# The delta rule's last group with its two pairs of heads interleaved, modulation sums moved out of the output projection's last quarter, and the feed-forward input scaled in another place

## The chip, the cores and the metric

The kernel runs on one core of a Trainium2 chip. The metric is device microseconds of one execution; lower is better. TensorE (PE) does the matmuls; its weight loads are listed apart as PEld. VectorE (DVE), ScalarE (ACT) and GpSimd (POOL) do the elementwise work. SyncE (SP), ACT and POOL issue DMA transfers, each in its own order. Every engine works through its instructions in a fixed order, and waits at an instruction until the semaphores it names have been reached.

## The reference, cut to what matters

One layer of a hybrid encoder block for one sequence of 256 tokens and a model width of 2048, all in fp32:

```python
mod = c_act @ ada_w + ada_b
shift_m, scale_m, gate_m, shift_f, scale_f, gate_f = split(mod, 6)
h = rms_norm(x, norm_mix_w) * (1 + scale_m) + shift_m
proj = h @ w_in                                  # all branch inputs and the merge gates
y_a = (sigmoid(a_o) * norm(bidirectional(mlstm, ...))) @ w_branch_a
y_b = (norm(bidirectional(gated_delta, ...)) * silu(b_z)) @ w_branch_b
x = x + gate_m * ((g_a * y_a + g_b * y_b) @ w_out)
hf = rms_norm(x, norm_ffn_w) * (1 + scale_f) + shift_f
gt, up = split(hf @ w_gate_up, 2)
x = x + gate_f * ((silu(gt) * up) @ w_down)
return rms_norm(x, norm_final_w)
```

The gated delta rule has 16 heads of width 128, the mLSTM 4 heads; the feed-forward is 5632 wide.

## The kernel before

**Weights.** Every projection is a job of the generator `tjob` or `fjob`. A weight tile `raw` of 1 MB is loaded by SP into one of 4 buffers, and in halves of 128x1024 it is split into a rounded part `wh` (ACT) and a remainder `wl` (DVE), with 3 buffers each. PE multiplies wh with the high and the low part of the input, and wl with the high part: 12 matmuls of 128x512 for each half. Each `next` of such a job issues one half. In names, o3_2_0 is the half from row 0 of weight tile 2 of job o3. The jobs for the merge gates are ma0 to ma3 and mb0 to mb3, those of the mLSTM branch a, v and o, those of the branch outputs ya and yb, the output projection is once more called o (o0 to o3, one for each quarter of the columns, its weights are `wo`), and the feed-forward has gt, up and d.

**The delta rule.** The 16 heads go in four groups of four, each as two pairs. `gdn_phase2(g, p)` is a generator of nine steps for one pair: p1 to p4 (small matmuls that invert blocks, each followed by DVE and ACT work), pa, pb and pc (matmuls with the triangular blocks, each followed by a scaling on ACT or a subtraction on DVE), po (12 matmuls, then a norm: squares on ACT, a root, four scalings `on` on DVE), and px (transposes, evicted by ACT as `obt` and stored to memory). Each step waits for the step ahead of it on another engine. Between steps the loop calls `stream` (the input projections of later heads, and behind them jobs from the list `fills`), so that PE has other work. The lists `after` and `last` say how many half-jobs go behind each step. For the last group, g = 3, the stream holds fills alone: the remaining a jobs and ma3.

When the last group is done its pool of buffers is closed. The next stage uses the same memory, so its first instructions wait for the last pair's stores: `obh` and `obl` (the delta rule's output o4_0 to o4_3, read back from memory and split by ACT and DVE), the branch projection yb, and POOL's loads for the mLSTM (`mkq`, `vt`, `sgo`, `bc`, two heads ahead), which stand behind its load of o4_3. psc is the mLSTM's first matmul, pden and ph follow.

**Modulation sums.** `mod` is not computed on PE. For each block of 128 outputs, SP loads a 1 MB tile `ada` and one DVE instruction (line 127) multiplies it with the conditioning row and sums it up. The parts 2 to 5 of these sums are a background list: `sums(n)` issues n of them, and `pump`, called once for each weight tile of a job, issues one at every `every[0]`-th call. Part 4 (the feed-forward's scale) must be complete before `affn`, which scales the feed-forward's input. In the projection o, sums are issued behind chosen halves of each quarter.

**Into the feed-forward.** The last quarter of o finishes token block 0 first and then token block 1. For each, DVE does tm = acc_o * gm and x1 += tm (`residual`), ACT the squares, and `token_rstd` a reduce (DVE), a root (ACT) and a reciprocal (DVE). Then `normed` scales x1 into xn, a quarter of the columns at a time and two buffers in all; `moved` transposes it on PE (pxn), scales it to `hf` (DVE, or ACT for most odd blocks) and rounds it to hfh (ACT); `low` makes hfl (DVE). The first feed-forward job, gt0, is issued in between, block pair by block pair.

Tile's scheduler places the instructions of each engine by its own model of time; those wrapped in `order(...)` keep their program order among themselves.

Of the kernel before, what the change touches and what calls it, by code (L numbers as in the profile page):

```python
# [52 lines left out]
def hybrid_block(ctx: ExitStack, tc: tile.TileContext, xr, nfr, crow, pk_d, cst_d, ada2, ada4, win0, winb, wint, wba, wbb, wo, wgu, wd, out, dbg=None):  # L53
# [809 lines left out]
    after = (0, 1, 2, 1, 2, 2, 2, 2, 4, 0)  # L863
    last = (0, 1, 2, 1, 2, 2, 1, 1, 3, 0)

# [25 lines left out]
    for g in range(4):  # L891
# [9 lines left out]
        every[0] = (0, 2, 2, 2)[g]  # L901
        for p in range(2):
            pieces = stream(4 * g + 2 * p + 4)
            if g == 3:
                o4s += [o_load(i, op, 3) for i in ((0, 1), (2,))[p]]
            for n in range(1, 10):
                next(pairs[p], None)
                if p == 0:
                    next(blocks, None)
                for _ in range(after[n] if g < 3 else last[n]):  # L910
                    next(pieces)
            for _ in pairs[p]:
                pass

            if g < 3:
                while 4 * g + 2 * p + 5 not in heads:
                    next(pieces)
        if g < 3:
# [233 lines left out]
    for g in range(4):  # L1152
# [33 lines left out]
    def normed(q, t, parts, eng):  # L1186
        if q not in xns:
            xns[q] = hp.tile([P, 2, 512], F32, tag="sg", bufs=2, name=f"xn{q}")
        o, i = xns[q][:, t, parts], x1[:, t, q * 512 + parts.start : q * 512 + parts.stop]
        if eng is V:  # L1190
            order(V.tensor_scalar(o, i, rs1[:, t : t + 1], None, ALU.mult))
        else:
            order(S.activation(o, i, AF.Copy, scale=rs1[:, t : t + 1]))
# [20 lines left out]
    for t in range(2):  # L1214
        normed(0, t, slice(256, 512), S)
    moved(0)
    moved(1)
# [5 lines left out]
    for b in range(2, KB, 2):  # L1223
# [4 lines left out]
        next(gt0)  # L1228
        if b % 4 == 2 and b < 12:
            for t in range(2):  # L1230
# [163 lines left out]
```

## Time and profile before

| | |
|---|---|
| time, median of 3 runs | 1982.52 us (1982.24 to 1983.56) |
| the profiled execution's own time | 1979.27 us |
| its span | 1977.3 us |
| mean granted PE clock | 0.988 |
| PE busy | 1918.9 us (97%) |
| PEld busy | 1705.5 us (86%) |
| DVE busy | 1402.5 us (71%) |
| ACT busy | 1022.7 us (52%) |
| POOL busy | 96.9 us (5%) |
| read from memory | 469.16 MB |

All times inside the profile count from the start of its span. The last group's first step, p1, stands at 861.69; the output projection o ends at 1253.71; the feed-forward begins at 1262.28 with gt0 and ends with the span. The granted clock is the share of TensorE's full speed that it was given.

### The profile page before, as it was taken

To read this page: it belongs to the slowest core of one execution; us is meant where nothing else is said; L and a number is where in the kernel's file an instruction comes from. 1 tells how busy PE (TensorE), PEld (TensorE's weight loads), DVE (VectorE), ACT (ScalarE), POOL (GpSimd) and SP (SyncE) were. 2 spreads that over 40 slices of the span, in tenths; PEclk is the share of its full clock that TensorE was granted. 3 is DMA by queue.
4 is the path that set the end of the run, shared out by engine and by line. 5 is a ranking of instruction groups with operands and counts; after the bars stand their busy time and mean duration, and the time that the engine had idled before them with its cause. 6 is when DMAs were issued, how large, how long until landed. Compare 5 with 4: busy or idle time off the path is not lost.

```text
span 1977.3 us, 27036 instructions
## 1 busy us (share of the span) xinstructions
PE 1918.9 (97%) x10352; PEld 1705.5 (86%) x10352; DVE 1402.5 (71%) x2091; ACT 1022.7 (52%) x1568; POOL 96.9 (5%) x185
## 2 busy tenths in 40 slices
PE   8999999999999999999799999799999999999997
PEld 6887889989989998998688888688888888888886
DVE  5779887878988996965587769766666655555554
ACT  3146657855765686465454444554444444444443
POOL 0000300110100011000200000000000000000000
PEclk9999999999999999999799999899999999999999
DMA  9996665567667765885677679466766765566563
GB/s 400 420 383 194 222 223 192 167 203 283 228 199 247 281 214 191 310 303 190 234 291 266 249 288 419 182 234 235 265 244 237 262 246 193 205 240 203 202 206 114
DMA packets 78675, 487.76 MB, mean 247 GB/s; under 512 B 10265, under 2 KB 15681, under 8 KB 23889
## 3 DMA queue, kind: packets, MB, share of 16 engines
q1 hardware_dynamic: 63360, 450.95, 62.2%
q0 software_dynamic: 7872, 19.99, 4.4%
q10 hardware_dynamic: 7314, 15.10, 2.1%
q8 instruction: 81, 1.33, 0.3%
q14 instruction: 48, 0.39, 0.1%
HBM read 469.16 MB, written 16.83 MB: 246 GB/s over the span
## 4 chain that ended last, share of the span: by engine, by line
PE 73%; DVE 11%; DMA 9%; ACT 4%; issue 2%; POOL 0%; SPq 0%; ACTq 0%; DVEq 0%; POOLq 0%
DMA ra<-ada 5%; PE acc_up L215 4%; PE acc_up L218 4%; PE acc_up L216 4%; PE acc_d L216 4%; PE acc_d L215 4%; PE acc_d L218 4%; PE acc_gt L216 4%; PE acc_gt L215 4%; PE acc_gt L218 4%; PE acc_o L218 2%; PE acc_o L216 2%; PE acc_o L215 2%; PE acc_a L175 2%; PE acc_b L175 2%
## 5 line engine op out<-in xcount | busy, mean ns | idle before, releaser
L198 DVE TENSOR_TENSOR wl_d<-raw_d,wh_d 128x1024 fp32r<-128x1024 f32 x88 | 107.8, 1225 | 102.7 <-ACT wh_d L197 102.7
L127 DVE SCALAR_TENSOR_TENSOR ada<-ada,crow 128x2048 f32<-128x2048 f32 x64 | 146.5, 2289 | 43.6 <-DMA ada<-ada 43.5
L198 DVE TENSOR_TENSOR wl_up<-raw_up,wh_up 128x1024 fp32r<-128x1024 f32 x88 | 107.5, 1225 | 95.9 <-ACT wh_up L197 95.9
L197 ACT ACTIVATE wh_d<-raw_d 128x1024 fp32r<-128x1024 f32 x88 | 93.0, 1057 | 130.5 <-PE acc_d L216 125.3
L198 DVE TENSOR_TENSOR wl_gt<-raw_gt,wh_gt 128x1024 fp32r<-128x1024 f32 x88 | 107.7, 1224 | 72.4 <-ACT wh_gt L197 68.2
L197 ACT ACTIVATE wh_gt<-raw_gt 128x1024 fp32r<-128x1024 f32 x88 | 92.9, 1056 | 120.7 <-PE acc_gt L216 73.2
L197 ACT ACTIVATE wh_up<-raw_up 128x1024 fp32r<-128x1024 f32 x88 | 93.0, 1056 | 118.2 <-PE acc_up L216 71.7
L215 PE MATMUL acc_gt<-wh_gt,hfh 128*128 128x512 f32 x352 | 135.2, 384 | 0.0
L216 PE MATMUL acc_gt<-wh_gt,hfl 128*128 128x512 f32 x352 | 134.6, 382 | 0.0
L175 PE MATMUL acc_b<-hh,wh_b 128*128 128x256 f32 x576 | 134.6, 276 | 0.0
L175 PE MATMUL acc_b<-hl,wh_b 128*128 128x256 f32 x576 | 134.6, 277 | 0.0
L215 PE MATMUL acc_up<-wh_up,hfh 128*128 128x512 f32 x352 | 133.5, 379 | 0.0
L216 PE MATMUL acc_up<-wh_up,hfl 128*128 128x512 f32 x352 | 133.5, 379 | 0.0
L216 PE MATMUL acc_d<-wh_d,ffl 128*128 128x512 f32 x344 | 130.4, 379 | 0.0
L215 PE MATMUL acc_d<-wh_d,ffh 128*128 128x512 f32 x344 | 130.4, 379 | 0.0
L530 PE MATMUL first<-x,raw 128*128 128x256 f32 x512 | 114.5, 382 | 7.5 <-ACT x L523 6.8
L530 PEld LDWEIGHTS first<-x,raw 128*128 128x128 f32 x512 | 96.1, 190 | 25.9 <-ACT x L523 12.4
L175 PEld LDWEIGHTS acc_b<-hl,wh_b 128*128 128x128 f32 x576 | 110.6, 192 | 0.4
L175 PEld LDWEIGHTS acc_b<-hh,wh_b 128*128 128x128 f32 x576 | 110.5, 192 | 0.5
L197 ACT ACTIVATE wh_o<-raw_o 128x1024 fp32r<-128x1024 f32 x64 | 67.1, 1054 | 58.9 <-PE acc_o L216 35.5
L218 PE MATMUL acc_gt<-wl_gt,hfh 128*128 128x512 f32 x352 | 95.3, 385 | 0.0
L171 ACT ACTIVATE wh_b<-raw_b 128x1024 fp32r<-128x1024 f32 x72 | 76.1, 1058 | 37.1 <-PE acc_b L175 22.8
(384 smaller groups left out, 5018.4 us busy)
## 6 DMA issues: line engine op xcount, KB each, us to landing
ada<-ada SPq DMA_DIRECT2D x64, 1024.0 KB, 5.8
raw_gt<-wgu SPq DMA_DIRECT2D x44, 1024.0 KB, 5.0
raw_up<-wgu SPq DMA_DIRECT2D x44, 1024.0 KB, 4.9
raw_d<-wd SPq DMA_DIRECT2D x44, 1024.0 KB, 4.9
raw_b<-winb SPq DMA_DIRECT2D x36, 1024.0 KB, 5.0
ra<-ada SPq DMA_DIRECT2D x32, 1025.0 KB, 15.8
raw<-win SPq DMA_DIRECT2D x16, 1024.0 KB, 17.1
raw_z<-wint SPq DMA_DIRECT2D x16, 1024.0 KB, 5.2
```

The lines of the kernel that those rows point to most:

```text
L127: V.scalar_tensor_tensor(raw, raw, 1.0, row_c[:, :D], ALU.mult, ALU.mult, accum_out=mod[:, c0 + b : c0 + b + 1])
L171: S.activation(wh, raw[:, k0 : k0 + 8], AF.Copy)
L175: PE.matmul(o, wh[:, k], both(x, k0 + k).rearrange("p a b -> p b a"), start=k0 + k + i == 0, stop=False)
L197: order(S.activation(wh, raws[u][:, k0 : k0 + 2], AF.Copy), hold)
L198: order(V.tensor_tensor(wl, raws[u][:, k0 : k0 + 2], wh.bitcast(F32), ALU.subtract), hold)
L215: order(PE.matmul(ps[t], tok(xh, kk, t), turns(wh[:, k]), start=kk == 0, stop=False), early and steps > 1)
L216: PE.matmul(ps[t], tok(xl, kk, t), turns(wh[:, k]), start=False, stop=False)
L218: PE.matmul(ps[t], tok(xh, kk, t), turns(wl[:, k]), start=False, stop=kk == last)
L530: PE.matmul(first[o], raw[:, o], x[:, b], start=b == 0 and o % 2 == 0, stop=b == KB - 1 and o % 2 == 1)
```

## The change

It has four parts.

1. In the last group the two pairs are driven by one loop of 13 rounds: the first pair takes a step in rounds 1 to 9, the second in rounds 5 to 13. Two half-jobs follow each round (26 in all, as many as with the list `last`).
2. `every[0] = 0` moves from ahead of the last ya job to behind it, so that two sums are issued within the last ya jobs.
3. In o, sums stand behind halves 2, 4, 6, 7 of the first quarter, behind 1, 3, 5, 7 of the second and third, and behind none of the last, apart from the call that empties the list there.
4. In `normed`, xn1 is made by POOL instead of ACT and issued ahead of the transposes; xn2 and xn3 are issued one pass of the loop sooner.

```diff
-    last = (0, 1, 2, 1, 2, 2, 1, 1, 3, 0)
...
-        for p in range(2):
+        for p in range(2) if g < 3 else ():
             pieces = stream(4 * g + 2 * p + 4)
-            if g == 3:
-                o4s += [o_load(i, op, 3) for i in ((0, 1), (2,))[p]]
             for n in range(1, 10):
                 next(pairs[p], None)
                 if p == 0:
                     next(blocks, None)
-                for _ in range(after[n] if g < 3 else last[n]):
+                for _ in range(after[n]):
                     next(pieces)
...
+        if g == 3:
+            flow = [stream(4 * g + 4 + 2 * p) for p in range(2)]
+            for n in range(1, 14):
+                next(pairs[0], None)
+                if n > 4:
+                    next(pairs[1], None)
+                if n < 6:
+                    next(blocks, None)
+                if g == 3 and n in (1, 6):
+                    o4s += [o_load(i, op, 3) for i in ((0, 1), (2,))[n > 1]]
...
+                for _ in range(2):
+                    next(flow[n > 8])
...
         if g == 3:
-            every[0] = 0
             while len(background) > 2:
                 sums()
             row_store(2, ml, 0.5)
         run(y_a(g, mgh, mgl))
+    every[0] = 0
...
-            if i in ((4, 6, 7), (1, 2, 4, 6), (1, 2, 4, 6), (1, 2, 4))[g]:
+            if i in ((2, 4, 6, 7), (1, 3, 5, 7), (1, 3, 5, 7), ())[g]:
                 sums()
             if g == 3 and i == 4:
                 sums(P)
...
-        if eng is V:
-            order(V.tensor_scalar(o, i, rs1[:, t : t + 1], None, ALU.mult))
+        if eng is not S:
+            order(eng.tensor_scalar(o, i, rs1[:, t : t + 1], None, ALU.mult))
...
     for t in range(2):
         normed(0, t, slice(256, 512), S)
+    for t in range(2):
+        normed(1, t, slice(0, 512), G)
     moved(0)
...
-        if b % 4 == 2 and b < 12:
+        if b % 4 == 0 and b < 12:
             for t in range(2):
                 normed(b // 4 + 1, t, slice(0, 512), S)
```

What this does to the engines' orders, at three places. In the names, 3_1 is the last group's second pair, and a trailing number is a buffer's. Lines above 860 are up to 18 higher in the changed file.

PE at the end of the merge job ma3, before: the pair's last steps stand behind the job, and the branch projection yb0 behind them.

```order
L218 MATMUL acc_ma3_1_9176<-wl_ma3_3_2_9326,hh_131 128x512
L775 MATMUL pb_3_1_8773<-z3_1_8728,gg14_7349 128x128 x2
L775 MATMUL pb_3_1_8773<-z3_1_8728,gg15_7594 128x128 x2
L763 MATMUL pc_3_1_8799<-r3_1_8729,UL_1115 128x128
L764 MATMUL pc_3_1_8799<-r3_1_8729,UL_1115 128x128
L785 MATMUL po_3_1_8826<-z3_1_8728,at14_7350 128x128
```

PE at the same place, after: from the pair's last px, inside the job's last half, to the first matmul of yb0.

```order
L796 MATMUL px_3_1_8809<-cst_78,on15_8824 128x128 x2
L215 MATMUL acc_ma3_0_9175<-wh_ma3_3_2_9325,hh_131 128x512
L216 MATMUL acc_ma3_0_9175<-wh_ma3_3_2_9325,hl_132 128x512
L215 MATMUL acc_ma3_1_9176<-wh_ma3_3_2_9325,hh_131 128x512
L216 MATMUL acc_ma3_1_9176<-wh_ma3_3_2_9325,hl_132 128x512
L218 MATMUL acc_ma3_0_9175<-wl_ma3_3_2_9326,hh_131 128x512
L218 MATMUL acc_ma3_1_9176<-wl_ma3_3_2_9326,hh_131 128x512
L218 MATMUL acc_ma3_0_9175<-wl_ma3_3_2_9326,hh_131 128x512
L218 MATMUL acc_ma3_1_9176<-wl_ma3_3_2_9326,hh_131 128x512
L215 MATMUL acc_yb0_0_9366<-wh_yb0_0_0_9370,obh_8961 128x512
```

All of the pair's matmuls now stand ahead of the job's last 8; pb, pc, po and px were 24 behind it.

DVE at the same place, before: ada3_7 is a modulation sum, r, so and on belong to the pair, obl is the next stage.

```order
L127 SCALAR_TENSOR_TENSOR ada3_7_9505,mod_88<-ada3_7_9505,crow_76 128x2048
L198 TENSOR_TENSOR wl_yb0_0_2_9387<-raw_yb0_0_9368,wh_yb0_0_2_9386 128x1024
L776 TENSOR_TENSOR r3_1_8729<-vv14_7345,pb_3_1_8773 128x256
L776 TENSOR_TENSOR r3_1_8729<-vv15_7590,pb_3_1_8773 128x256
L810 SCALAR_TENSOR_TENSOR so3_1_8840<-so3_1_8840,sm14_7322 128x2
L810 SCALAR_TENSOR_TENSOR so3_1_8840<-so3_1_8840,sm15_7567 128x2
L814 RECIPROCAL so3_1_8840<-so3_1_8840 128x4
L819 SCALAR_TENSOR_TENSOR on14_8841<-po_3_1_8826,so3_1_8840,sz3_7794 128x128 x2
L819 SCALAR_TENSOR_TENSOR on15_8842<-po_3_1_8826,so3_1_8840,sz3_7794 128x128 x2
L933 TENSOR_TENSOR obl_8962<-o4_0_8217,obh_8961 128x1024
```

DVE there, after:

```order
L819 SCALAR_TENSOR_TENSOR on14_8823<-po_3_1_8808,so3_1_8822,sz3_7794 128x128 x2
L819 SCALAR_TENSOR_TENSOR on15_8824<-po_3_1_8808,so3_1_8822,sz3_7794 128x128 x2
L198 TENSOR_TENSOR wl_ma3_3_0_9310<-raw_ma3_3_9307,wh_ma3_3_0_9309 128x1024
L198 TENSOR_TENSOR wl_ma3_3_2_9326<-raw_ma3_3_9307,wh_ma3_3_2_9325 128x1024
L198 TENSOR_TENSOR wl_yb0_0_0_9371<-raw_yb0_0_9368,wh_yb0_0_0_9370 128x1024
L127 SCALAR_TENSOR_TENSOR ada3_7_9505,mod_88<-ada3_7_9505,crow_76 128x2048
L198 TENSOR_TENSOR wl_yb0_0_2_9387<-raw_yb0_0_9368,wh_yb0_0_2_9386 128x1024
L949 TENSOR_TENSOR obl_8962<-o4_0_8228,obh_8961 128x1024
```

The pair's norm now stands ahead of the merge job's last splits. The sum ada3_7 and the split behind it, for which SP's next two raw_yb loads wait, still follow the merge job's last split.

DVE at the end of o, before: tmss is the tm of `residual`, with the token block and the quarter in its name.

```order
L1113 TENSOR_TENSOR tmss1_10970_0_3_11585<-acc_o3_0_11445,gm_10968 128x512
L127 SCALAR_TENSOR_TENSOR ada4_14_11481,mod_88<-ada4_14_11481,crow_76 128x2048
L1114 TENSOR_TENSOR x1_10966<-x1_10966,tmss1_10970_0_3_11585 128x512
L1123 TENSOR_REDUCE rs1_10971<-ss1_10970 128x1
L1125 RECIPROCAL rs1_10971<-rs1_10971 128x1
L1113 TENSOR_TENSOR tmss1_10970_1_3_11604<-acc_o3_1_11446,gm_10968 128x512
L1114 TENSOR_TENSOR x1_10966<-x1_10966,tmss1_10970_1_3_11604 128x512
L127 SCALAR_TENSOR_TENSOR ada4_15_11502,mod_88<-ada4_15_11502,crow_76 128x2048
L1123 TENSOR_REDUCE rs1_10971<-ss1_10970 128x1
L129 TENSOR_TENSOR mod_88<-mod_88,pk_77 128x16
L1167 SCALAR_TENSOR_TENSOR affn_10972<-mod_88,pk_77 128x16
L1125 RECIPROCAL rs1_10971<-rs1_10971 128x1
```

DVE there, after:

```order
L127 SCALAR_TENSOR_TENSOR ada4_15_11405,mod_88<-ada4_15_11405,crow_76 128x2048
L129 TENSOR_TENSOR mod_88<-mod_88,pk_77 128x16
L1183 SCALAR_TENSOR_TENSOR affn_10978<-mod_88,pk_77 128x16
L198 TENSOR_TENSOR wl_o3_3_0_11560<-raw_o3_3_11557,wh_o3_3_0_11559 128x1024
L198 TENSOR_TENSOR wl_o3_3_2_11564<-raw_o3_3_11557,wh_o3_3_2_11563 128x1024
L198 TENSOR_TENSOR wl_gt0_0_0_11570<-raw_gt0_0_11567,wh_gt0_0_0_11569 128x1024
L1129 TENSOR_TENSOR tmss1_10976_0_3_11585<-acc_o3_0_11452,gm_10974 128x512
L1130 TENSOR_TENSOR x1_10972<-x1_10972,tmss1_10976_0_3_11585 128x512
L1139 TENSOR_REDUCE rs1_10977<-ss1_10976 128x1
L1141 RECIPROCAL rs1_10977<-rs1_10977 128x1
L1129 TENSOR_TENSOR tmss1_10976_1_3_11604<-acc_o3_1_11453,gm_10974 128x512
L1130 TENSOR_TENSOR x1_10972<-x1_10972,tmss1_10976_1_3_11604 128x512
```

The last sum and `affn` now stand ahead of o3's last weight splits, and no sum stands among the residual's instructions.

POOL from the mLSTM's last gate row to the end, after (before, the two rows of line 1207 were not there):

```order
L141 DMA row_d2_92<-rowsm2_10794 16x128
L144 DMA gm_10974<-row_d2_92 128x2048
L1207 ISA
L1207 TENSOR_SCALAR xn1_11633<-x1_10972,rs1_10977 128x512 x2
L141 DMA row_d5_93<-rowsm5_15051 16x128
L144 DMA gf_15046<-row_d5_93 128x2048
```

[...]

More of the change, by code (lines that the diff above doesn't have):

```diff
@@ L913, in hybrid_block @@
                 pass
-            if g < 3:
-                while 4 * g + 2 * p + 5 not in heads:
-                    next(pieces)
+            while 4 * g + 2 * p + 5 not in heads:
+                next(pieces)
+        if g == 3:
[8 more added lines that the diff above has]
+                    o4s += [o_load(i, op, 3) for i in ((0, 1), (2,))[n > 1]]
+                if n == 9 and g < 3:
+                    while 4 * g + 5 not in heads:
+                        next(flow[0])
+                for _ in range(2):
+                    next(flow[n > 8])
+            for pair in pairs:
+                for _ in pair:
+                    pass
+            while g < 3 and 4 * g + 7 not in heads:
+                next(flow[1])
         if g < 3:
```

## The prediction

> **What bounds the kernel now.** I read the page first (busy shares, slices of the clock), then the windows table stage by stage, then in order of time each engine around the two places where TensorE is not busy.
>
> ```profile
> PE 1918.9 (97%) x10352; PEld 1705.5 (86%) x10352; DVE 1402.5 (71%) x2091; ACT 1022.7 (52%) x1568; POOL 96.9 (5%) x185
> ...
> PEclk9999999999999999999799999899999999999999
> ```
>
> TensorE is busy for 97% of the span; its granted clock sags in only two slices. The windows table (stretch; then length, busy time and, in brackets, count of PE, PEld, DVE, ACT, POOL; last the granted clock, the DMA share, GB/s) shows what they are:
>
> ```profile
> 860.00:934.70 74.70, 74.70 (x501) 69.78 (x500) 42.21 (x48) 44.91 (x87) 0.00 (x0) 1.00 0.66 236
> 934.70:951.77 17.07, 6.66 (x46) 5.31 (x44) 4.75 (x13) 7.82 (x21) 0.39 (x1) 0.83 0.51 171
> 951.77:965.24 13.47, 9.76 (x32) 7.11 (x32) 7.67 (x10) 5.01 (x5) 7.49 (x13) 0.83 0.96 348
> 966.40:980.06 13.66, 13.17 (x44) 11.35 (x44) 7.24 (x19) 6.16 (x10) 2.10 (x4) 0.50 0.48 160
> 1253.71:1260.51 6.80, 0.01 (x2) 0.01 (x1) 5.54 (x14) 2.49 (x8) 0.00 (x0) 0.71 0.00 0
> 1260.51:1291.57 31.06, 26.21 (x117) 21.25 (x117) 20.05 (x32) 20.55 (x36) 0.00 (x0) 0.90 0.32 105
> 1291.57:1950.00 658.43, 658.43 (x3096) 577.38 (x3095) 378.73 (x349) 294.30 (x312) 1.05 (x2) 1.00 0.65 228
> ```
>
> Until 934.70 and from 1291.57 on PE never pauses, so only these gaps can be won: 934.70 to 965.24, where the second pair's last steps stand without fill work and the mLSTM's loads follow, and 1253.71 to 1291.57, from the last output projection into the feed-forward. A full-clock 128x512 matmul comes every 658.43 / 3096 = 0.213 us.
>
> **Part 1, the pairs.** PE, ACT, POOL and SP at the first gap, in order of time (start, length; in brackets the idle time before and its releaser):
>
> ```profile
> 934.70 0.61 PE L775 MATMUL pb<-z,gg 128*128 128x128 f32 x4
> 937.56 0.68 PE L775 MATMUL pb<-z,gg 128*128 128x128 f32 x4 [2.26 <-DVE r L776]
> 941.40 0.39 PE L785 MATMUL po<-z,at 128*128 128x128 f32 x2
> 942.52 0.39 PE L790 MATMUL po<-z,at 128*128 128x128 f32 x2
> 946.25 0.73 PE L796 MATMUL px<-cst,on 128*128 128x128 f32 x2 [3.34 <-DVE on L819]
> 947.54 0.69 PE L796 MATMUL px<-cst,on 128*128 128x128 f32 x2 [0.56 <-ACT obt L798]
> 951.77 1.22 PE L215 MATMUL acc_yb<-wh_yb,obh 128*128 128x512 f32 x2 [3.53 <-ACT obh L932]
> 965.24 2.62 PE L957 MATMUL psc<-mkq 128*128 128x256 f32 x8 [3.33 <-DMA mkq<-kq_d]
> ...
> 935.62 1.08 ACT L332 ACTIVATE ev_ma<-acc_ma 128x512 f32<-128x512 f32 x2
> 950.66 2.95 ACT L932 ACTIVATE obh<-o 128x1024 fp32r<-128x1024 f32 x3 [1.92 <-DMA ob_d<-obt]
> 951.38 0.80 POOL L886 DMA_DIRECT2D o<-ob_d  x1 [100.38 <-DMA ob_d<-obt]
> 935.85 1.47 SPq L193 DMA_DIRECT2D raw_yb<-wbb  x2
> ```
>
> At 934.70 the last merge job is used up; the pair's pb, pc, po and px then wait for DVE and ACT with nothing between. The quoted orders put these 24 small matmuls among the merge job. Nothing is added; PE pays for them in time, (942.52 - 941.40) / 5 = 0.224 each, 5.4 us, so the merge job ends at 940.1. The last px now stands 8 matmuls (1.7 us) ahead of that and ends at 938.4, against 947.54 + 0.69 = 948.23 before: 9.8 us sooner. Everything that waited for the pair's store moves with it: obh followed px by 2.43 us, POOL's load of the last o by 3.15 (941.6 now). On ACT the eviction ev_ma now stands between px's eviction and obh; it needs the merge job's end and 1.1 us, so obh starts at 941.2 instead of 940.8, and PE starts yb (1.11 behind obh) at 942.3. That costs nothing: PE's next wait, for mkq, ends later.
>
> That wait is where part of the gain goes. psc needs the second mkq, behind five other loads on POOL's queue, and 951.77 to 965.24 ran DMA at a share of 0.96. Until now other traffic had passed by then:
>
> ```profile
> q1 hardware_dynamic: 252, 1.93, 64.9%
> q10 hardware_dynamic: 140, 0.52, 14.2%
> ...
> gtb<-mb_d SPq DMA_DIRECT2D x2, 512.0 KB, 4.3
> o<-ob_d POOLq DMA_DIRECT2D x1, 512.0 KB, 7.0
> ```
>
> These are the queues from 935 to 944 (two raw_yb by SP, the store ma_d by ACT; packets, MB, share) and the landing times from 950 to 966. The raw_yb loads wait for the modulation sum and the split behind the merge job's last split, so they move with the job's end, to about 941: beside POOL's loads, no longer 15 us ahead of them. SP's gtb landed in 4.3 us where POOL's o took 7.0, so I count raw_yb as served first: 1.93 MB at 348 GB/s, 5.5 us. psc then starts 9.8 - 5.5 = **4.3 us** sooner. Bounds: 9.8 if POOL's loads go first; 2.8 if the store counts too (2.45 MB, 7.0 us).
>
> Behind psc the clock was at 0.50 for 13.66 us, and this window lies just ahead:
>
> ```profile
> 962.99:966.40 3.41, 1.16 (x5) 1.05 (x6) 3.41 (x9) 0.51 (x1) 2.08 (x4) 1.00 1.02 394
> ```
>
> PE idled there for 2.25 of 3.41 us, and the clock fell. Both waits for mkq stay, and grow, so I take the same slow stretch: 0. Bounds: -6.8 us if it does not fall (half of 13.66), +1.7 if it lasts one such window more.
>
> The second pair's earlier steps, too, now stand among other jobs' matmuls, in PE's fixed order. I cost their waits at nothing: in 860.00 to 934.70 both pairs' steps stood so, and PE idled 0.00. This cover goes if both pairs' ACT and DVE work together comes late (rival 3).
>
> **Part 2, the sums.** Each is one 1 MB load on SP and one DVE pass. The total stays; two move into the last branch projection, the rest of o's last quarter into its first three. There DVE waits for its loads, as it did once already:
>
> ```profile
> 1127.83 2.29 DVE L127 SCALAR_TENSOR_TENSOR ada<-ada,crow 128x2048 f32<-128x2048 f32 x1 [3.81 <-DMA ada<-ada]
> 1132.52 1.13 PE L218 MATMUL acc_ya<-wl_ya,hah 128*128 128x512 f32 x4 [0.49 <-DVE wl_ya L198]
> ```
>
> A sum 3.81 us late, with weight splits behind it on DVE, cost PE 0.49. Two more: I take **0.5 us** of loss (bounds 0 and 1.0). At the end of o the two sums leave DVE:
>
> ```profile
> 1251.77 2.28 DVE L127 SCALAR_TENSOR_TENSOR ada<-ada,crow 128x2048 f32<-128x2048 f32 x1
> 1253.98 0.69 DVE L1114 TENSOR_TENSOR x<-x,tmss 128x512 f32<-128x512 f32 x1
> 1255.45 0.16 DVE L1123 TENSOR_REDUCE rs<-ss 128x1 f32<-128x4 f32 x1 [0.79 <-ACT tmss L1115]
> 1256.05 0.67 DVE L1113 TENSOR_TENSOR tmss<-acc_o,gm 128x512 f32<-128x512 f32 x1
> 1257.37 2.28 DVE L127 SCALAR_TENSOR_TENSOR ada<-ada,crow 128x2048 f32<-128x2048 f32 x1
> 1259.58 0.15 DVE L1123 TENSOR_REDUCE rs<-ss 128x1 f32<-128x4 f32 x1
> 1260.51 1.97 PE L1200 MATMUL pxn<-cst,xn 128*128 128x128 f32 x8 [6.79 <-ACT xn L1193]
> ```
>
> Without the first, x of token block 0 starts 1253.98 - 1251.77 = 2.21 sooner, and with it the second block's tmss (1253.84; its PSUM is ready at 1253.71) and x (0.7 later, 1254.55). The first block's reduce came 1.47 behind its x, so the second's comes at 1256.02 instead of 1259.58: the second sum no longer stands ahead of it. Transposes, and all behind, start **3.56 us** sooner, at 1256.95. SP's queue loses two loads ahead of the gate weights, which were there in time anyway.
>
> **Part 3, the scaled input.** xn1 goes from ACT to POOL, xn2 and xn3 each one step earlier on ACT.
>
> ```profile
> 1267.24 0.33 PE L1200 MATMUL pxn<-cst,xn 128*128 128x128 f32 x1 [1.54 <-ACT xn L1193]
> 1268.22 0.54 DVE L1206 TENSOR_SCALAR hf<-pxn,affn,mod 128x256 f32<-128x256 f32 x1 [0.39 <-PE pxn L1200]
> 1272.24 0.54 DVE L1206 TENSOR_SCALAR hf<-pxn,affn,mod 128x256 f32<-128x256 f32 x1
> 1291.09 0.54 DVE L1206 TENSOR_SCALAR hf<-pxn,affn,mod 128x256 f32<-128x256 f32 x1
> ...
> L388 POOL MEMSET tr<- 128x512 f32 x1 | 0.5, 529 | 0.0
> ```
>
> PE's waits for xn are gone, but not their whole length is won, because hf, hfh, hfl and the weight splits alternate on DVE and ACT: the one step without an xn wait took 1272.24 - 1268.22 = 4.02 us, five took 1291.09 - 1268.22 = 22.87. Five at 4.02 are 20.1: **2.8 us**, and the first hf no longer waits its **0.4**. The matmuls of a step (12 x 0.213) fit under 4.02, so PE follows. POOL's two scalings have no row; the nearest is a memset of 128x512, 0.53. The second can start when the reciprocal is there, 1256.02 + (1256.05 - 1255.45) = 1256.6, and is wanted at 1267.24 - 3.56 - 1.54 = 1262.1: 5.5 us of cover, so I cost it at 0. Below, it cannot gain; above, each us beyond the cover is lost. Behind it on POOL stand only the last gate row's store and load, near the end of the feed-forward.
>
> The idle time ahead of the transposes shrinks from 6.80 to about 3.2 us. After 2.25 idle us of 3.41 the clock fell (row above), so I expect it to fall here too and take nothing. [...]
>
> **Sum.** 4.3 - 0.5 + 3.56 + 2.8 + 0.4 = 10.5 us. The profiled execution took 1979.27, so 1968.8 there; the median of the runs shown is 3.25 above it, at 1982.52, and the forecast is put on that: 1972.0.
>
> **Rivals.** (1) POOL's loads go ahead of raw_yb: 9.8 instead of 4.3, **1966.5**. For it: no row fixes how the DMA engines divide themselves between queues; against it: gtb against o. (2) The pair part wins nothing, through small waits of the interleaved steps or the store and loads together: 6.2 remain, **1976.3**. For it: DMA is full either way; against it: from 934.70 to 951.77 PE was busy for 6.66 of 17.07 us, and that idle time lay ahead of every load. (3) Slower: the interleaved steps wait on PE. Where no fill work covered them a waiting step cost 2.26 and 3.34, 2.8 on average; four such waits eat the gain, and eight of the two pairs' eighteen steps would give 22, **1994**. Against it: PE's 74.70 busy of 74.70. [...]
>
> **Chances.** Forecast 0.60 (1969 to 1975.5), (1) 0.15, (2) 0.12, (3) 0.05, (4) 0.05, 0.03 for none of these. The range 1966 to 1977.5 takes in the forecast and rivals (1) and (2), which are its ends. What a measurement can tell is about 0.2%, 4 us: forecast, (1), (2) and a part of (4) are faster by more, 0.90; same 0.05; slower 0.05.
>
> **What would show it.** After: no PE wait between pb and px of the last pair; obh near 941; the second psc near 961 with DMA full before it (if near 955, rival 1); the transposes about 3.2 us behind o's last matmul; hf every 4.0 us; no PE wait for xn. I am wrong if PE idles inside the merge job, if psc does not come sooner at all, or if PE waits for POOL.

## The result, and the profile after

The changed kernel took 1972.62 us (median of five runs, 1971.84 to 1977.0), the kernel before in the same session 1983.56 (1982.24 to 1986.4). The ratio is 0.9949, with a 95% interval from 0.9935 to 0.9962: 10.1 us faster (7.5 to 12.9). The forecast was 1972.0, in a range from 1966 to 1977.5.

The total fits, but not its parts. The changed kernel's profiled execution took 1972.29, with a span of 1970.4, 6.9 us less than the span before, where the steps of the forecast gave 10.5. (The profiled execution of before, 1979.27, lies 3 us below the shortest of its five runs here.) The lines of the page that answer to those shown of before:

```profile
PE 1917.9 (97%) x10352; PEld 1701.8 (86%) x10352; DVE 1400.5 (71%) x2091; ACT 1020.3 (52%) x1566; POOL 100.3 (5%) x187
...
PEclk9999999999999999999899999999999999999999
```

TensorE's busy time fell by 1.0 us; nearly all of the gain is idle time. One of the two dips of the clock is gone (one slice of forty below 9, where before had two). To see where the time went, I cut both kernels at the same matmuls: the last matmul of the last z job, yb's first, yb's first behind the first 18 products ph of heads 0 and 1, the first of ya, the first and last of o. These are the five stretches of before in the windows table (length; then busy time of PE, PEld, DVE, ACT, POOL; clock, DMA share, GB/s):

```profile
773.20:951.77 178.57, 168.16 (x1052) 154.03 (x1050) 117.16 (x188) 96.96 (x173) 9.04 (x15) 0.98 0.70 251
951.77:980.67 28.90, 24.70 (x83) 20.00 (x83) 16.68 (x31) 11.78 (x16) 10.38 (x18) 0.69 0.72 253
980.67:1076.19 95.52, 95.52 (x454) 83.37 (x453) 75.74 (x96) 48.02 (x66) 1.60 (x3) 0.98 0.74 275
1076.19:1169.02 92.83, 92.06 (x444) 79.86 (x443) 67.55 (x81) 43.23 (x55) 0.51 (x1) 1.00 0.68 244
1169.02:1253.33 84.31, 83.80 (x392) 73.19 (x391) 73.39 (x73) 36.85 (x46) 0.55 (x1) 1.00 0.98 399
```

And the same of the changed kernel, then the stretch into the feed-forward, the feed-forward itself, and the merge job with the interleaved pairs:

```profile
772.01:941.50 169.49, 166.88 (x1051) 153.30 (x1049) 116.42 (x188) 95.25 (x172) 9.95 (x16) 1.00 0.70 250
941.50:973.09 31.59, 22.80 (x82) 17.86 (x83) 14.63 (x30) 9.58 (x14) 9.50 (x17) 0.78 0.85 313
973.09:1070.21 97.12, 95.89 (x453) 83.33 (x453) 75.41 (x97) 50.45 (x69) 1.60 (x3) 0.98 0.73 271
1070.21:1169.43 99.22, 94.33 (x444) 80.80 (x443) 73.28 (x85) 43.26 (x55) 0.51 (x1) 0.98 0.69 249
1169.43:1253.43 84.00, 83.81 (x392) 73.15 (x391) 72.99 (x75) 37.58 (x48) 0.55 (x1) 1.00 0.92 375
...
1257.27:1284.60 27.33, 25.73 (x116) 20.01 (x117) 18.09 (x31) 19.57 (x35) 1.56 (x1) 0.94 0.35 116
1284.60:1943.00 658.40, 658.40 (x3096) 577.07 (x3096) 379.89 (x351) 294.21 (x312) 1.10 (x2) 1.00 0.65 229
860.00:938.79 78.79, 78.72 (x539) 73.33 (x537) 44.70 (x59) 48.83 (x103) 0.00 (x0) 1.00 0.63 226
```

The pairs bring 9.1 us to yb's first matmul; then 2.7 are lost in the first heads, 1.6 in yb, 6.4 in ya; o is level. At o's last matmul the changed kernel is 0.1 us *later* than before (1253.43 against 1253.33). Only the two parts behind it are left in this profile: 3.3 us ahead of the transposes and 3.7 into the feed-forward. TensorE and ScalarE in order of time at the places that the forecast named, and where the lead went:

```profile
936.85 0.38 PE L796 MATMUL px<-cst,on 128*128 128x128 f32 x2
940.39 1.06 ACT L948 ACTIVATE obh<-o 128x1024 fp32r<-128x1024 f32 x1
941.50 0.70 PE L215 MATMUL acc_yb<-wh_yb,obh 128*128 128x512 f32 x2 [2.55 <-ACT obh L948]
952.67 3.35 PE L973 MATMUL psc<-mkq 128*128 128x256 f32 x8 [3.20 <-DMA mkq<-kq_d]
959.95 3.65 PE L973 MATMUL psc<-mkq 128*128 128x256 f32 x8 [3.92 <-DMA mkq<-kq_d]
1026.24 1.13 PE L218 MATMUL acc_yb<-wl_yb,obh 128*128 128x512 f32 x4 [1.23 <-DVE wl_yb L198]
1089.53 1.17 PE L216 MATMUL acc_ya<-wh_ya,hal 128*128 128x512 f32 x2 [1.79 <-DVE hal L1040]
1142.21 1.13 PE L218 MATMUL acc_ya<-wl_ya,hah 128*128 128x512 f32 x4 [1.41 <-DVE wl_ya L198]
1154.53 0.70 PE L218 MATMUL acc_ya<-wl_ya,hah 128*128 128x512 f32 x2 [1.69 <-DVE wl_ya L198]
1257.27 1.97 PE L1216 MATMUL pxn<-cst,xn 128*128 128x128 f32 x8 [3.46 <-ACT xn L1209]
```

The pair's last px waits for nothing. In ya there are three waits for VectorE, 4.9 us, where before had two, of 0.28 and 0.49. VectorE there and at o's end, and GpSimd:

```profile
1138.72 2.29 DVE L127 SCALAR_TENSOR_TENSOR ada<-ada,crow 128x2048 f32<-128x2048 f32 x1 [3.66 <-DMA ada<-ada]
1149.85 2.29 DVE L127 SCALAR_TENSOR_TENSOR ada<-ada,crow 128x2048 f32<-128x2048 f32 x1 [4.28 <-DMA ada<-ada]
...
1256.33 0.16 DVE L1139 TENSOR_REDUCE rs<-ss 128x1 f32<-128x4 f32 x1 [0.79 <-ACT tmss L1131]
1257.11 1.73 POOL L1207 TENSOR_SCALAR xn<-x,rs 128x512 f32<-128x512 f32 x1 [1.22 <-DVE rs L1141]
1264.52 0.54 DVE L1222 TENSOR_SCALAR hf<-pxn,affn,mod 128x256 f32<-128x256 f32 x1
1284.60 0.54 DVE L1222 TENSOR_SCALAR hf<-pxn,affn,mod 128x256 f32<-128x256 f32 x1
```

The two sums that moved into ya wait in VectorE's order for loads that are 3.66 and 4.28 us late; the weight splits queue behind them, and TensorE behind those. Both stand in ya's second half. Cut at ya's middle (its 193rd matmul of 384), the windows table has from yb's first matmul to there and from there to o's first, in before:

```profile
951.77:1124.96 173.19, 168.71 (x768) 145.26 (x769) 131.38 (x175) 83.92 (x114) 11.98 (x21) 0.94 0.73 265
1124.96:1169.02 44.06, 43.57 (x210) 37.97 (x209) 28.58 (x31) 19.11 (x22) 0.51 (x1) 1.00 0.66 235
```

and in the changed kernel:

```profile
941.50:1122.42 180.92, 169.12 (x768) 144.20 (x769) 130.77 (x175) 83.94 (x115) 11.10 (x20) 0.94 0.73 269
1122.42:1169.43 47.01, 43.91 (x210) 37.78 (x209) 32.55 (x35) 19.36 (x22) 0.51 (x1) 1.00 0.72 259
```

So 2.95 us are lost where the moved sums stand, and 7.7 ahead of them, from yb's first matmul on, where no sum was moved. At the end of o, nothing stands ahead of the second reduce. Five hf steps take 1284.60 - 1264.52 = 20.08 us, 4.02 each.

### The profile page after: what moved, and what is told of

The parts are those of the page before. It is cut to its first block, busy times and chain, and to the rows that moved or that the text cites. A ratio compares the mean times of both kernels' runs of the same rounds, so it can differ in the third digit from the quotient of the medians.

```text
span 1970.4 us, 27039 instructions
## 1 busy us (share of the span) xinstructions
PE 1917.9 (97%) x10352; PEld 1701.8 (86%) x10352; DVE 1400.5 (71%) x2091; ACT 1020.3 (52%) x1566; POOL 100.3 (5%) x187
## 4 chain that ended last, share of the span: by engine, by line
PE 79%; DMA 8%; DVE 7%; ACT 3%; issue 2%; ACTq 0%; POOL 0%; SPq 0%; DVEq 0%; POOLq 0%
PE acc_b L175 5%; DMA ra<-ada 4%; PE acc_up L215 4%; PE acc_up L218 4%; PE acc_up L216 4%; PE acc_d L216 4%; PE acc_d L218 4%; PE acc_d L215 4%; PE acc_gt L216 4%; PE acc_gt L215 4%; PE acc_gt L218 4%; PE acc_o L218 3%; PE acc_o L215 3%; PE acc_o L216 3%; PE acc_b L177 2%; PE acc_a L175 2%
```

## The experiments

Each kernel was timed against the kernel before on its own chip, and profiled once. The table has the same stretches (us), from each profile; "first heads" is from yb's first matmul to yb's first behind the first 18 ph products of heads 0 and 1, "to FFN" from the first transpose to the first matmul of the up projection.

| kernel | z to yb | first heads | yb | ya | o | o's end | to FFN | median, us | ratio to before (95%) |
|---|---|---|---|---|---|---|---|---|---|
| before | 178.57 | 28.90 | 95.52 | 92.83 | 84.31 | 7.17 | 31.06 | | |
| changed | 169.49 | 31.59 | 97.12 | 99.22 | 84.00 | 3.84 | 27.33 | 1972.62 | 0.9949 (0.9935 to 0.9962) |
| p_only | 169.16 | 31.39 | 99.36 | 93.58 | 84.46 | 7.18 | 31.07 | 1978.04 | 0.9975 (0.9960 to 0.9989) |
| s_only | 178.24 | 30.07 | 96.07 | 96.08 | 84.06 | 3.75 | 31.07 | 1980.99 | 0.9991 (0.9978 to 1.0004) |
| x_only | 181.05 | 28.84 | 95.51 | 92.92 | 84.15 | 7.26 | 27.34 | 1979.84 | 0.9986 (0.9974 to 0.9998) |
| p_x | 169.16 | 31.60 | 99.83 | 92.28 | 84.32 | 7.27 | 27.33 | 1975.64 | 0.9959 (0.9943 to 0.9975) |
| o_dense | 170.25 | 34.75 | 95.54 | 93.51 | 85.11 | 7.27 | 27.33 | 1973.97 | 0.9954 (0.9936 to 0.9971) |
| after_rate1 | 187.78 | 26.42 | 103.50 | 100.55 | 83.98 | 3.85 | 27.32 | 1992.27 | 1.0044 (1.0029 to 1.0059) |
| sums_early | 181.66 | 31.02 | 96.14 | 95.16 | 84.34 | 3.85 | 27.31 | 1982.54 | 0.9990 (0.9979 to 1.0002) |
| sums_early_kq | 182.38 | 23.88 | 94.08 | 94.68 | 84.67 | 3.84 | 27.31 | 1974.88 | 0.9956 (0.9940 to 0.9973) |
| after_kq | 169.94 | 28.22 | 95.53 | 98.06 | 84.19 | 3.84 | 27.34 | 1971.17 | 0.9938 (0.9921 to 0.9955) |
| after_kq_gt | 169.63 | 26.34 | 93.84 | 97.43 | 84.14 | 3.85 | 27.33 | 1965.24 | 0.9906 (0.9890 to 0.9922) |
| after_kq2_gt | 169.16 | 26.06 | 93.85 | 96.14 | 84.56 | 3.84 | 27.33 | 1965.67 | 0.9905 (0.9889 to 0.9922) |
| px_kq_gt | 169.16 | 26.44 | 93.84 | 94.53 | 84.49 | 7.25 | 27.33 | 1961.13 | 0.9887 (0.9870 to 0.9903) |

How far one profile goes: up to the last z matmul all kernels but the two with early sums run the same code, yet that point came between 772.0 and 780.8 us; the stage from there to yb, with the old order, took 178.24 to 181.05. So a single span says less than the stretches, and the ratios decide on totals. The same order can also differ by 3 us over one stretch, as the table at the end of the next section shows.

### One part at a time

p_only takes the stagger alone, s_only the sums alone, x_only the scaled input alone, p_x the first and the last:

```diff
 # p_only, on before: the last group's two pairs in one loop (first hunks of the change)
-        for p in range(2):
+        for p in range(2) if g < 3 else ():
...
+            for n in range(1, 14):
+                next(pairs[0], None)
+                if n > 4:
+                    next(pairs[1], None)
...
 # s_only, on before
-            every[0] = 0
             while len(background) > 2:
...
+    every[0] = 0
...
-            if i in ((4, 6, 7), (1, 2, 4, 6), (1, 2, 4, 6), (1, 2, 4))[g]:
+            if i in ((2, 4, 6, 7), (1, 3, 5, 7), (1, 3, 5, 7), ())[g]:
 # x_only, on before
+    for t in range(2):
+        normed(1, t, slice(0, 512), G)
...
-        if b % 4 == 2 and b < 12:
+        if b % 4 == 0 and b < 12:
```

> Only the pairs of the last group are staggered; the sums and the scaled input stay as before. In the changed kernel the lead over the kernel before was 10.3 us at the first yb matmul, 7.6 behind the first two mLSTM heads, and 0.1 below zero at the output projection. Theory A (the sums that were moved into ya take the lead away): here the late sums of ya are absent, so 3 to 6 of the 7.6 us survive to the end: 4 to 6 us faster than before. Theory B (the stages behind the mLSTM run at the pace of their loads, so any lead is given back there): the output projection's first matmul wait comes at the same time as before, 1198, and the whole is within 1 us of before. Both: yb's first matmul about 9 to 10 us sooner, the second psc 4 to 5 us sooner.

Measured: 5 us faster by the ratio (2 to 8). The stage to yb is 9.4 us shorter, as in the changed kernel. The first heads take 2.5 more and yb 3.8 more; ya and o keep their length. Theory B falls for o, which takes 84.0 to 85.1 us in every kernel, whenever it starts, and in the total. But its idea holds ahead of o: 3.8 of the 6.9 us then left are lost in yb, without any sum moved, and between the two profiles 2.3 us of the lead reach o. This is where, VectorE and then TensorE of p_only in order of time:

```profile
1022.11 2.29 DVE L127 SCALAR_TENSOR_TENSOR ada<-ada,crow 128x2048 f32<-128x2048 f32 x1 [3.62 <-DMA ada<-ada]
...
1028.60 1.13 PE L218 MATMUL acc_yb<-wl_yb,obh 128*128 128x512 f32 x4 [1.88 <-DVE wl_yb L198]
```

A sum of yb itself, 3.62 us late; before, TensorE came there later and did not wait. Behind the wait the clock was at half for a while: from 1029.78 on, eleven matmuls of 128x512 took 4.06 us, 1.7 more than at the 0.215 apiece of those ahead.

> Only the modulation sums are moved: two into the last branch projection, none in o's last quarter. Theory A: the two sums in ya are waited for on their loads and cost TensorE about 3 us in two waits near 1145 and 1157, less the 0.5 of the one wait that was there; the transposes behind o start 3.3 to 3.6 us sooner relative to o's end; sum between 0 and 1 us faster than before. Theory B: the output projection stands at the loads' pace either way and takes up the loss in ya, so 3.3 us faster than before.

Measured: no difference that the runs can tell. ya grew by 3.25 us and o's end shrank by 3.42. Only 1.9 of the 3.25 lie in ya's second half, where the moved sums stand (0.95 and 0.37 us of new waits there); the rest is a wait for hal of 1.59 us instead of 0.28 in the first half, ahead of them. So theory A has the end right and the price in ya a little high (about 2.5 forecast); B's gain of 3.3 us lies within the interval too, but o, where it should come from, shrank by only 0.3.

> Only the scaled feed-forward input comes sooner (xn1 on GpSimd, xn2 and xn3 one step earlier on ScalarE). My step: hf steps at 4.0 us instead of 4.0 to 4.7, 3.2 us faster. With the clock's sag at 1277 gone too, as in the changed kernel, up to 3.8. [...]

Measured: 2.8 us faster by the ratio (0.4 to 5.2); the stretch to the feed-forward 3.72 us shorter. TensorE has no wait for xn1.

> The changed kernel with the sums left where they were before. Theory A: faster than the changed kernel in its middle (lead at o about 3 to 6 us instead of -0.1) but 3.3 us slower at o's end: 7.5 to 10 us faster than before, level with the changed kernel to 2 us. Theory B: the lead is gone at o as well, so only the scaled input's 3.8 us are left.

Measured: 8.1 us faster (5.0 to 11.3), level with the changed kernel. The middle was only partly as A has it: ya is free of the moved sums (92.28), but yb took 4.3 us more than before.

The same kernels, cut at ya's middle (us). Up to there, kernels that differ only in the sums and in the scaled input run the same instructions in the same order on every engine by the names in the traces (but for one gtb load that o_dense issues a little later):

| kernel | last z matmul to ya's middle | of this, from yb's first matmul on | ya's middle to o | sums that start in this last stretch |
|---|---|---|---|---|
| before | 351.77 | 173.20 | 44.06 | 1 |
| x_only | 354.15 | 173.11 | 44.16 | 1 |
| s_only | 354.45 | 176.22 | 45.99 | 3 |
| p_only | 349.51 | 180.35 | 43.98 | 1 |
| p_x | 348.85 | 179.69 | 44.01 | 1 |
| o_dense | 349.77 | 179.52 | 44.29 | 1 |
| changed | 350.42 | 180.92 | 47.01 | 3 |
| px_kq_gt | 339.65 | 170.49 | 44.32 | 1 |
| after_kq_gt | 339.90 | 170.27 | 47.34 | 3 |

The first column gives the stagger's worth with three profiles of the old order and four of the new: 353.5 and 349.6 on average, 3.8 us, where yb's first matmul came 9.8 sooner. The last stretch gives the price of the two moved sums: 1.9 us in s_only (less x_only or before), 2.7 to 3.0 in the changed kernel, 3.0 in after_kq_gt.

### Where else to put the sums

o_dense leaves the sums out of ya's last quarter and asks for them in o's first three quarters; after_rate1 asks for a sum at every chunk in the last group's stage; sums_early asks for three in the last z job and inversion:

```diff
 # o_dense, on before with the stagger and the scaled input
-            if i in ((4, 6, 7), (1, 2, 4, 6), (1, 2, 4, 6), (1, 2, 4))[g]:
+            if i in ((2, 4, 6, 7), (1, 2, 4, 6, 7), (1, 2, 4, 6), ())[g]:
 # after_rate1, on the changed kernel
-        every[0] = (0, 2, 2, 2)[g]
+        every[0] = (0, 2, 2, 1)[g]
 # sums_early, on the changed kernel
-            every[0] = 0
+            every[0] = 4 if g == 2 else 0
             invert(g + 1)
...
         if g == 3:
+            every[0] = 0
             while len(background) > 2:
...
-    every[0] = 0
```

> The changed kernel with its two late sums of ya put into o's first three quarters (13 of the places there instead of 12, none in ya's last stretch, none in o's last quarter). So far: from the first ya matmul to the first of o took 92.8 us before, 96.1 with the sums alone moved, 99.2 in the changed kernel; o's matmuls took 84.0 to 84.5 everywhere, and DMA was full there. Theory A (the two sums in ya are what costs): ya's stage falls to 92.5 to 94, o's stays within 1 us of 84, o's end keeps its 3.8 us to the transposes; 3 to 6 us faster than the changed kernel. Rival C (ya in the changed kernel is long because it starts earlier and its loads do not): ya's stage stays at 96 to 99, level with the changed kernel. Rival D: the two sums only move their cost into o, whose DMA is full and whose VectorE is busy for 9 to 10 of 10 us: o's stage grows by 3.

Measured: ya fell from 99.22 to 93.51, o grew by 1.1. But o's end is 7.27, not 3.8: the scheduler, which sets VectorE's order, left the last two sums between the residuals, whatever the list asked for. VectorE of o_dense, in order of time:

```profile
1250.41 2.28 DVE L127 SCALAR_TENSOR_TENSOR ada<-ada,crow 128x2048 f32<-128x2048 f32 x1
...
1256.10 2.28 DVE L127 SCALAR_TENSOR_TENSOR ada<-ada,crow 128x2048 f32<-128x2048 f32 x1
```

So it became the changed kernel with its sums back in o's last quarter, and the total is level with the changed kernel's. It confirms the 3.4 us of o's end. Of ya's 5.7 us it gives the moved sums only the 2.7 of the second half; in the first half, where both kernels run the same order, they differ by 3.0 all the same. (Its first heads took 3.2 us more than the changed kernel's in this profile, with the clock at half for longer: its ph products came 0.43 us apart up to 977.28, in the changed kernel up to 970.07.)

> The changed kernel with a sum at every weight chunk, instead of every other, in the last group's stage of the delta rule (TensorE busy, DMA at 0.62, VectorE at 0.5): about eight sums come there that came in yb, ya and o, and ya and o run out of them. Theory A: ya's stage falls to 91.5 to 93, o's stays near 84, DMA no longer full in o; 4 to 8 us faster than the changed kernel, if the last group's stage (169.2 to 169.5 from the last z matmul to yb's first) does not grow. Rival E: the sums wait there for their loads ahead of the pairs' VectorE steps, and TensorE's waits for them lengthen that stage by 3 us or more; then level or slower.

Measured: 20 us slower than the changed kernel. Rival E: the stage to yb took 187.78 us, 18 more. Theory A was not put to the test in ya: the sums ran out in o, which had 5 instead of 11, while six still started in ya, and yb and ya took 103.50 and 100.55. Its windows table, and then TensorE in order of time: DMA is full where the sums crowd, TensorE pauses for 4.5 us, and the pair's waits at the end are back.

```profile
830.00:890.00 60.00, 55.45 (x276) 47.83 (x274) 49.69 (x64) 22.30 (x27) 2.85 (x5) 1.00 0.97 369
```

```profile
956.14 0.50 PE L796 MATMUL px<-cst,on 128*128 128x128 f32 x2 [3.44 <-DVE on L819]
```

The sums delay the pairs' steps until the merge job no longer reaches over them. This is the forecast's rival 3, brought about by a full DMA and a busy VectorE rather than by the stagger.

> The changed kernel with three sums put in the last z job and inversion (where the kernel had none from 723 to 814), so that ya's last quarter and o's last quarter both have none. So far ya's stage took 99.2 and 98.1 us with the two late sums, 92.3 to 93.6 without; o's end to the transposes 3.8 without sums there, 7.2 with. Theory A (each of the two places costs what it was seen to cost, and only there): ya 92 to 94 and o's end 3.8 in one kernel, 5 to 6 us faster than the changed kernel, about 1967. Rival E' (as with a sum at every chunk: sums ahead of latency-bound VectorE steps hold TensorE up): the stage from before the z job to yb's first matmul grows by 3 us or more, and nothing is won.

Measured: rival E' again. Three sums ahead of the group cost 12.2 us of the stage to yb; o's end (3.85) did what theory A says and ya nearly (95.16 for 92 to 94), and the total is level with before. The last px of the pair waits once more, in TensorE's order of time:

```profile
950.49 0.66 PE L796 MATMUL px<-cst,on 128*128 128x128 f32 x2 [5.19 <-DVE on L819]
```

### The loads of the first heads

```diff
 # after_kq, on the changed kernel: GpSimd's queue o, mkq, bc, mkq, bc, vt, sgo, vt, sgo
-    cores = steps(mlstm(0), mlstm(1))
...
     o4s.append(o_load(3, ml, 1))
+    early = [kq_load(h) for h in range(2)]   # mkq and bc of a head
+    cores = steps(*(mlstm(h, early[h]) for h in range(2)))
 # after_kq_gt, besides: gtb0 and gtb1 on GpSimd's queue behind these
-        nc.sync.dma_start(gt, mb_d[g])
+        (G if g < 2 else nc.sync).dma_start(gt, mb_d[g])
 # after_kq2_gt, besides: both mkq ahead of both bc
 # sums_early_kq: sums_early with after_kq's edit;  px_kq_gt: p_x with after_kq_gt's two
```

> The changed kernel with GpSimd's queue in another order: the first two heads' mkq and bc ahead of both vt and sgo, so that the second mkq stands behind 1.8 MB of its queue (itself included) instead of 2.9. My step (the load's time goes by the bytes ahead of it, at 348 GB/s): second psc 3 us sooner, at 956 to 957 if yb starts at 941.5; 10.3 to 11.4 us from yb's first matmul to the first psc become 8 to 11. The stretch from yb's first matmul to the end of the first two heads' products (31.6 us) falls by 2 to 3, unless vt, now later, takes over the wait there (rival: 0, with a wait of the ph products).

Measured: the second mkq landed 15.43 us behind yb's first matmul instead of 18.40, the 3.0 expected. The second psc came at 16.05 instead of 18.44, only 2.4 sooner, because it now stands behind the first psc and not behind its load. The first heads are 3.4 us shorter. The time is 12 us below before (0.9938), too near the changed kernel's 0.9949 to tell them apart. In TensorE's order of time both psc now stand in one row:

```profile
959.78 6.59 PE L977 MATMUL psc<-mkq 128*128 128x256 f32 x16 [4.55 <-DMA mkq<-kq_d]
```

The first of them is 1.35 us later than in the changed kernel (12.51 behind yb's first against 11.17). The new order does not explain it, for the first mkq is second in the queue in both. GpSimd issued it 0.82 us later against yb's first matmul (0.33 behind it instead of 0.49 ahead); the rest is open.

> The same with the first heads' mkq and bc loaded ahead of vt and sgo, which shortened the stretch from yb's first matmul to the end of the first two heads' products from 31.6 to 28.2 us. If the two edits add up: 3 us faster than sums_early, 8 us faster than the changed kernel, about 1964. Rival: the lead is given back in yb and ya, as 1.6 to 4.3 us of the pairs' lead were; then level with sums_early.

Measured: 7.7 us faster than sums_early by the medians, more than the 3 expected, and not shown to differ from after_kq (0.9956 against 0.9938, the intervals overlap). The first heads fell by 7.1 us, yb by 2.1.

> after_kq with the first two gtb loads (1.05 MB) taken off SP's queue and put on GpSimd's, behind vt and sgo of the first heads. In the changed kernel they were issued together with o and mkq and landed after 10 us, as late as o's 9.6. My step (what stands in DMA at the same time, on whatever queue, delays mkq by its bytes): second psc up to 1.05 MB / 0.348 = 3 us sooner; from yb's first matmul to the second psc 13 instead of 16.05, and to the end of the first heads' products 25.5 to 27 instead of 28.2; the time 1 to 3 us below after_kq's 1971.2 unless yb gives it back. Rival (SP's queue is served beside GpSimd's without cost): 16 us as in after_kq.

Measured: 6 us faster than after_kq by the medians, at the same baseline to 3 us; 0.9906 against 0.9938. The second psc came at 14.65 instead of 16.05. It waits for the first psc in both, so the loads themselves are the better measure: from GpSimd's first issue, o, to the landing of the second mkq took 14.7 us instead of 15.9, and 14.2 in px_kq_gt. That is 1.2 to 1.7 us for the 3.0 that the bytes alone would give. So the two gtb loads on SP's queue had delayed mkq on GpSimd's by 1.2 to 1.7 us, about half of my estimate. (They were not only put on another queue: GpSimd issued them 12.5 and 13.7 us behind yb's first matmul, where SP had issued them about 1 ahead of it.) First heads, yb and ya of after_kq_gt in the windows table:

```profile
943.87:970.21 26.34, 21.06 (x82) 16.90 (x83) 17.43 (x32) 10.83 (x14) 10.54 (x19) 0.81 0.99 372
970.21:1064.05 93.84, 93.84 (x454) 82.14 (x452) 72.31 (x94) 48.42 (x65) 1.59 (x3) 1.00 0.76 280
1064.05:1161.48 97.43, 93.09 (x444) 79.48 (x443) 73.99 (x86) 44.64 (x58) 0.51 (x1) 1.00 0.71 254
```

In yb TensorE is busy throughout and the clock is 1.00: nothing of the lead is given back there. Why the sums of yb no longer hold it up is not settled: they still wait for their loads, for up to 5.91 us.

> The same with both mkq loads ahead of both bc loads (after_kq put bc of the first head ahead of the second mkq, and the first psc came 1.4 us later than in the changed kernel, 12.5 instead of 11.2 behind yb's first matmul). If bytes ahead decide: first psc back to 10 to 11, second 0.7 sooner than in after_kq_gt, but the scans of bc later, so no more than 1 us in the stretch to the end of the first heads' products; time level with after_kq_gt within 1.5 us.

Measured: level with after_kq_gt, as expected; the first psc at 10.89 instead of 11.30. The second mkq landed 1.1 us sooner, but the second psc, behind the first, came only 0.3 sooner for 0.7 expected.

> after_kq_gt with the sums left where the kernel before had them. From the stages so far: ya 92.3 to 93.6 us instead of 97.4, o's end to the transposes 7.2 instead of 3.85, so 0.5 to 2 us faster than after_kq_gt (1965.2): moving the sums is no gain by itself. Rival: the sums in ya cost only where VectorE was already late, and after_kq_gt has only 1.5 us of waits left there; then ya falls by 1.5 and this kernel is 2 us slower than after_kq_gt.

Measured: the fastest kernel of the study, 1961.13 us, 0.9887: 22.4 us faster than before (19.2 to 25.8) and about twice the gain of the changed kernel. Against after_kq_gt the intervals overlap, so that not moving the sums is at least no loss. Its ya took 2.9 us less, all of it in the second half, where the moved sums were; its o's end took 3.4 more. First heads, yb and ya of px_kq_gt:

```profile
944.05:970.49 26.44, 22.70 (x83) 18.43 (x84) 17.78 (x32) 10.83 (x14) 10.54 (x19) 0.74 1.01 376
970.49:1064.33 93.84, 93.84 (x453) 82.31 (x452) 72.18 (x94) 48.42 (x65) 1.59 (x3) 1.00 0.76 279
1064.33:1158.86 94.53, 92.59 (x444) 79.77 (x443) 70.13 (x82) 44.40 (x58) 0.51 (x1) 1.00 0.67 239
```

## Why the prediction was right, and where it was not

- **Pairs up to yb: right.** Forecast 9.5 us (yb at 942.3), measured 9.1 in the stage; obh at 940.39 for "near 941"; no wait between pb and px; TensorE busy for 78.72 of 78.79 us over the interleaved steps, which were costed at nothing.
- **The loads' collision: right in size.** Forecast 18.6 us from yb's first matmul to the second psc, measured 18.44. The net 4.3 came out as 13.47 - 18.44 + 9.08 = 4.1. The reason was half right: in after_kq the second mkq, further ahead in GpSimd's queue, landed 3.0 us sooner, and in after_kq_gt, without the two gtb loads beside it, it took 1.2 us less from GpSimd's first issue, not 3.0. raw_yb did not go first: in the changed kernel the two loads, issued 1.66 us ahead of yb's first matmul and 1.13 behind it, landed 4.28 and 14.72 us behind it, the second of them between GpSimd's first mkq (11.03) and second (18.40).
- **The clock behind psc: taken as unchanged, won 2.3.** The stretch from the second psc to the end of the ph products took 13.15 us instead of 15.42; the clock was at 0.50 there for twice 3.41 us (from 959.91 and 966.74), where before it was for 13.66 on end. p_only (13.15) and p_x (13.38) show the same; in o_dense the stretch took 16.06, so this gain is not one to count on.
- **Behind that, all was to move along: wrong by stages, nearly right in sum.** The forecast had no term for yb. With TensorE sooner, yb's own sums were late for it, and yb took 1.6 us more than before in this profile, 3.8 and 4.3 in p_only and p_x. o_dense, with the same order, lost nothing in yb but 5.9 in the first heads. At ya's middle the four staggered profiles are 3.8 us ahead of the three others, for a net forecast of 4.3; single profiles of the two kinds lie 1.4 to 5.6 us apart, so this holds on average only. The forecast also took only the two gaps for winnable, and did not look at yb, ya and o between them, where TensorE waited for VectorE for 1.3 us before and for 6.1 after.
- **The sums: the step that failed.** "I take 0.5 us of loss (bounds 0 and 1.0)" was measured, in the stretch where the moved sums stand, at 1.9 (s_only), 2.7 to 3.0 (the changed kernel less o_dense, p_only or p_x) and 3.0 (after_kq_gt less px_kq_gt). I had priced two more sums by the one wait of 0.49 that showed. The loads of the new ones are as late as that one's (3.66 and 4.28 against 3.81), but the splits behind them reach TensorE 1.4 and 1.7 us late, not 0.5; that there were fewer finished splits in hand by then is my reading, not shown. The other 3.4 of ya's 6.4 are no price of the move: they are the 1.79 us wait for hal in the first half, behind a sum 3.74 us late that stood there before as well (then 1.98 late), and 3.41 us at a clock of 0.50 that followed it (1089.62 to 1093.03).
- **o's end: right.** Forecast 3.56, measured 3.33, and 3.42 in s_only; TensorE idle 3.46 us there for "about 3.2".
- **The scaled input: right.** Forecast 3.2, measured 3.73; hf steps at 4.02. GpSimd's scaling took 1.73 us where I had put a memset's 0.53, and the cover of 5.5 us hid it. The first scaling began at 1254.32, 0.2 us behind its reciprocal.
- **The sum: right partly by luck.** The terms add up to 10.56, put down as 10.5. Stage by stage, the profile has 4.1 + 2.3 - 1.6 - 6.4 + 0.3 + 3.3 + 3.7 = 5.7, and 1.2 from ahead of the change. The timed runs have 10.1. Most of the 3 us between are likely owed to the one profile of before: x_only, which runs before's order as far as ya's middle, took 2.4 us more than it from z to there, and s_only 2.7. With the averages of the table above the sum is 3.8 - 3.0 + 0.3 + 3.3 + 3.7 = 8.1, within the interval of the timed runs (7.5 to 12.9). So the pairs, o's end and the scaled input were forecast about right, the sums were mis-sized by 1.4 to 2.5 us, and that the total agreed to 0.6 us is luck.

The rivals did not come: the second psc was at 959.95 and not 955 (1), the pair part wins alone, by 2 to 8 us in p_only (2), TensorE idles for only 0.07 us over the interleaved steps (3), and TensorE never waits for xn1 from GpSimd (4).

## What to carry to other kernels

Making TensorE earlier was a gain here only as far as the loads and the helper engines behind it were early too (9.8 us at yb were 3.8 at ya's middle): price a moved wait at the next two stages, not at its own. Price it from more than one profile: the same order took 173.1 to 176.2 us over one stretch. A sum that waited for its load held up the splits behind it in VectorE's order, and TensorE with them by 1.41 and 1.69 us, so the price of one more of them was not the stall that the last one showed (0.49) but the load's lateness (here near 4 us) less the lead that is left (that last part argued, not shown). And when a wait for DMA is uncovered, look at the order of the loads before anything else: two edits of a queue were worth about as much here as the whole change (0.9906 against 0.9949 with the sums moved, 0.9887 against 0.9959 without).

## What the hardware showed that I had not expected

In before a window of 3.41 us in which TensorE was busy throughout was followed by one at a clock of 0.50. These are the two in the windows table; the row behind them is TensorE's in order of time:

```profile
1051.80:1055.21 3.41, 3.41 (x29) 3.33 (x28) 3.41 (x4) 1.11 (x3) 0.00 (x0) 1.00 0.93 317
1055.21:1058.62 3.41, 3.41 (x10) 2.70 (x9) 0.84 (x7) 0.48 (x1) 0.00 (x0) 0.50 1.02 423
```

```profile
1052.17 2.73 PE L981 MATMUL pden<-ones,mdec 128*128 128x1 f32 x24
```

For 2.73 us the first of them was filled with 24 matmuls of one column each. The changed kernel has the same: 23 of them in its trace, 2.66 us in a window that was busy for 3.41 of 3.41 (from 1045.25), and 0.50 in the next (from 1048.66). In after_kq_gt the same 24 ran for 2.73 us (from 1041.71) without a fall of the clock, which was 1.00 over all of yb, and yb took 95.52 - 93.84 = 1.68 us less, half of 3.41. What made the difference is not shown. At o's end in the changed kernel, in its windows table, 3.41 us with 0.35 us of work stood ahead of the fall:

```profile
1253.46:1256.87 3.41, 0.35 (x2) 0.00 (x0) 1.86 (x6) 1.36 (x5) 1.57 (x1) 1.00 0.00 0
1256.87:1260.28 3.41, 3.01 (x11) 2.53 (x12) 2.64 (x7) 2.13 (x6) 1.73 (x1) 0.50 0.00 0
```

The forecast had expected this fall, from the 1.16 us of work in the 3.41 ahead of before's slow stretch behind psc.
